# A hybrid HGRN2 and pooling trunk: the channel mixing of the last pooled group behind the first two column tiles of g, its gate in the larger pool of tiles

## The chip, the core and the metric

The kernel runs on one core of a Trainium2 chip. The metric is the device time of one execution in microseconds (us); lower is better. The engines are TensorE (PE, with its weight loads PEld), VectorE (DVE), ScalarE (ACT), GpSimd (POOL) and SyncE (SP), which issues most of the loads.

## What is computed

The reference is one layer of a trunk with two token mixers on the same normalised input, 512 tokens by 2048 channels. Cut to what matters here:

```python
proj = h @ w_in[l]
q_a, f_a, v_a, z_a, v_b, z_b, g_a, g_b = jnp.split(proj, IN_SPLITS, axis=-1)
o_a = hgrn2_mixer(q_a, f_a, v_a, lb_all[l])
y_a = rms(o_a) * hgrn_norm[l] * jax.nn.silu(z_a)
y_b = pool_mixer(v_b, pool_w[l], pool_scale[l]) * jax.nn.silu(z_b)
merged = jax.nn.sigmoid(g_a) * (y_a @ w_proj_a[l]) + jax.nn.sigmoid(g_b) * (y_b @ w_proj_b[l])
x = x + gate * rmsnorm(merged @ w_out[l], norm_post[l])

# pool_mixer, group g of four, 256 channels each, window w in (2, 4, 8, 16)
pooled_g = trailing_mean(v_b[:, g], w) - v_b[:, g]
mixed_g = pooled_g @ pool_w[g]          # the channel mixing, 256 x 256
```

`hgrn2_mixer` is a gated linear recurrence over 8 heads of 128, worked in chunks of 64 tokens.

## The kernel before

Tiles hold 128 channels by 512 tokens. Products are in float32 precision by three matmuls: each factor is split into a rounded part `hi` and the rest `lo`, and `mm3` (L198) adds hi x hi, hi x lo and lo x hi. A piece of weights comes through `w_piece` (L181): a load on SyncE into a ring of four raw tiles, a cast to `hi` on ScalarE (L187), a subtraction to `lo` on VectorE or GpSimd in turn (L188), each into rings of four. `in2` (L347) makes two column tiles of the input projection from four pieces, `name_0`, `_4`, `_8` and `_12`, of 24 matmuls each: eight for each column tile's four rows of h, in threes.

TensorE runs its matmuls in the order in which the program writes them (L97 to 104). The other engines' rows are put in order by the scheduler when the program is built, by priority and by what each row waits for; on the chip each engine then follows its own fixed order. Two pools of tiles matter: `t_w` (10 tiles, tag "w", short-lived) and `t_s` (32 tiles, tag "s").

After the first half of the projection the eight heads of the recurrence, `hgrn(h)` (L387), run as generators in the gaps: `mm3` calls `tick`, and after D0 to D6 = 21, 11, 13, 10, 6, 5 and 6 calls the next step of the head in turn writes its few matmuls between those of the projection. The steps named here are, in this order: `po` (the pairs), `lv_2`, `lv_8` and `lv_32` (scores within blocks of 8, 32 and 64 tokens), `far`, `state`, `o`, and `ms` (the mean square). Before each, ScalarE takes exponentials (`E`, `qs`, `R`, `A`) and VectorE subtracts before and multiplies after them; `Y` and `X` are `R` and `A` times the small tile `G`, and `far` reads them. In `E_8`, `qs_8_0` and so on the number is the block size; with two numbers ahead (`E_5_8`) the first is the head.

In between come the four pooled groups (L849 to 853): `vb` of group gi by `in2`, the pooling sums in `pool_tile` (L590, to `pl_hi` and `pl_lo`), `zb` by `in2`, then `pool_group` (L609): the weights `pw`, for both halves m a silu of `zb` (`szb`, L614), six matmuls (`mix`, L618), the product `yb` (L620) and its store to DRAM by GpSimd (L621). Hgrn heads 3, 4 and 5 run beside groups 1, 2 and 3. Right behind group 3 begins g, `in2("g0_0")` (L879), then `za` (L874), whose silus gate the heads, and the rest of g, with a sigmoid on each tile (L894). Silu, exp, sigmoid, square root and logarithm are kept in different tables on ScalarE; where the table has to change, an ACT_TABLE_LOAD stands ahead of the activation.

Of the kernel before, what the change touches and what calls it, by code (L numbers as in the profile page):

```python
# [12 lines left out]
AF = mybir.ActivationFunctionType  # L13
# [21 lines left out]
def trunk(ctx, tc, x, c, w_ada, b_ada, norm_pre, norm_post, w_in, lower_bounds, hgrn_norm,  # L35
          pool_w, pool_scale, w_proj_a, w_proj_b, w_out, out):
    nc = tc.nc
# [15 lines left out]
    def t_s(name, dt=F32):  # L53
        return act.tile([P, S], dt, tag="s", bufs=32, name=name)

    def t_w(name, n=S, dt=F32):
        return act.tile([P, 544], dt, tag="w", bufs=10, name=name)[:, :n]

    def t_ps(name):
        return ps.tile([P, S], F32, tag="ps", name=name)  # L60
# [4 lines left out]
    def t_pg(name):  # L65
        return pg.tile([P, S], F32, tag="pg", name=name)
# [4 lines left out]
    def paced(hi):  # L71

        if wsum_steps:
            dst, src, kw = wsum_steps.pop(0)
            with tc.issue_after(last_pool[0]):
                t = ins_of(nc.gpsimd.tensor_copy(token, hi[:, 0, 0:1].bitcast(F32)))  # L76
            with tc.issue_after(t):
                last_pool[0] = ins_of(nc.gpsimd.dma_start(dst, src, max_dma_last_dim=1024, **kw))  # L78

    def load(dst, src):  # L80

        if last_load[0] is None:
            d = nc.sync.dma_start(dst, src)
        else:
            with tc.issue_after(last_load[0]):
                d = nc.sync.dma_start(dst, src)
        last_load[0] = ins_of(d)
# [4 lines left out]
    def ins_of(d):  # L92
        return getattr(d, "ins", d)
# [38 lines left out]
    def finish_heads(n):  # L132
        while steps and len(heads_done) < n:
            tick(1)
# [46 lines left out]
    def w_piece(name, src, k0, nk, c0, n, eng=None):  # L181

        raw = ring.tile([P, nk, n], F32, tag="raw", bufs=4, name=f"{name}_raw")
        load(raw, src[k0 * P:(k0 + nk) * P, c0:c0 + n].rearrange("(k p) n -> p k n", p=P))
        hi = ring.tile([P, nk, n], F32R, tag="whi", bufs=4, name=f"{name}_hi")
        lo = ring.tile([P, nk, n], F32R, tag="wlo", bufs=4, name=f"{name}_lo")
        last_w[0] = ins_of(nc.scalar.copy(hi, raw))  # L187
        (eng or (nc.gpsimd if steps and next(turn) else nc.vector)).tensor_sub(lo, raw, hi.bitcast(F32))  # L188
        paced(hi)
        return hi, lo  # L190
# [7 lines left out]
    def mm3(o, wh, wl, xh, xl, first, last):  # L198
        matmul(o, wh, xh, first, False)
        matmul(o, wh, xl, False, False)  # L200
        matmul(o, wl, xh, False, last)
        if in_order[0]:
            tick()
# [139 lines left out]
    def proj2(name, src, nk, c0, xh, xl, outs):  # L343
        for k0 in range(0, nk, 4):
            cols(f"{name}_{k0}", src, k0, 4, c0, xh, xl, outs, 0, nk - 1)

    def in2(name, c0):  # L347
        outs = [t_ps(f"{name}_ps0"), t_ps(f"{name}_ps1")]
        proj2(name, w_in, KT, c0, hh, hl, outs)
        return outs  # L350
# [227 lines left out]
    def gate_a(h, p):  # L578
        sz = t_w(f"sza_{h}")
        nc.scalar.activation(sz, p, AF.Silu)  # L580
        sz_a[h] = sz

    def finish_a(h):
        y = o_sb[h]
        nc.vector.scalar_tensor_tensor(y, y, vec[:, R_HN + h:R_HN + h + 1], sz_a[h], op0=ALU.mult, op1=ALU.mult)
        last_pool[0] = ins_of(nc.gpsimd.dma_start(y_dram[0][h], y))
# [3 lines left out]
    def pool_tile(i, p):  # L590

        w = WINDOWS[i // 2]
        v = t_w(f"vb_{i}", 528)
        nc.vector.memset(v[:, 0:16], 0.0)
        nc.scalar.copy(v[:, 16:528], p)
        cur, n, lo = v, 1, 0
        while n < w:
            nxt = t_w(f"vb_{i}_{n}", 528)
            lo += n
            nc.vector.tensor_add(nxt[:, lo:528], cur[:, lo:528], cur[:, lo - n:528 - n])  # L600
            cur, n = nxt, 2 * n
        if w > 1:
            nc.vector.scalar_tensor_tensor(cur[:, 16:16 + w - 1], cur[:, 16:16 + w - 1], float(w),
                                           inv_pos[:, 0:w - 1], op0=ALU.mult, op1=ALU.mult)
        pl = t_w(f"pl_{i}")
        nc.vector.scalar_tensor_tensor(pl, cur[:, 16:528], 1.0 / w, v[:, 16:528], op0=ALU.mult, op1=ALU.subtract)
        pooled[i] = split(f"pl_{i}", pl, t_s)

    def pool_group(gi, zp):  # L609
        hi, lo = w_piece(f"pw_{gi}", pool_w[gi], 0, 2, 0, 256)  # L610
        for m in range(2):
            i = 2 * gi + m
            sz = t_w(f"szb_{i}")
            nc.scalar.activation(sz, zp[m], AF.Silu)  # L614
            mx = t_pg(f"mix_{i}")
            for k in range(2):
                ph, pl = pooled[2 * gi + k]
                mm3(mx, hi[:, k, m * P:(m + 1) * P], lo[:, k, m * P:(m + 1) * P], ph, pl, k == 0, k == 1)  # L618
            y = t_w(f"yb_{i}")
            nc.vector.scalar_tensor_tensor(y, mx, vec[:, R_PS + i:R_PS + i + 1], sz, op0=ALU.mult, op1=ALU.mult)  # L620
            nc.gpsimd.dma_start(y_dram[1][i], y)  # L621
# [3 lines left out]
    def gate_rows(j, k):  # L625

        if k == 0:
            gate[j] = t_w(f"gate_{j}")
        t = t_w(f"gw_{j}_{k}")
        load(t, w_ada[k * P:(k + 1) * P, 2 * D + j * S:2 * D + (j + 1) * S])  # L630
        if k == 0:
            nc.vector.tensor_scalar(gate[j], t, c_act[:, 0:1], None, op0=ALU.mult)
        else:
            nc.vector.scalar_tensor_tensor(gate[j], t, c_act[:, k:k + 1], gate[j], op0=ALU.mult, op1=ALU.add)  # L634

    def gate_finish(j):

        acc = gate[j]
        br = t_w(f"bg_{j}")
        load(br[0:1, :], b_ada[:, 2 * D + j * S:2 * D + (j + 1) * S])  # L640
        nc.vector.tensor_add(acc[0:1, :], acc[0:1, :], br[0:1, :])
        np_b = t_w(f"npost_{j}")
        load(np_b, norm_post[:, j * S:(j + 1) * S].to_broadcast([P, S]))
        gp = t_pg(f"gate_ps_{j}")
        hi, lo = split(f"gate_{j}", acc, lambda name, dt: t_w(name, S, dt))
        matmul(gp, ones_v, hi, True, False)
        matmul(gp, ones_v, lo, False, True)
        nc.vector.scalar_tensor_tensor(acc, gp, float(P), np_b, op0=ALU.mult, op1=ALU.mult)
# [195 lines left out]
    for h in (4, 6):  # L844
        o2 = in2(f"q{h}", OFF_Q + h * P)
# [3 lines left out]
    for gi in range(4):  # L849
        o2 = in2(f"vb{gi}", OFF_VB + gi * 256)  # L850
        pool_tile(2 * gi, o2[0]); pool_tile(2 * gi + 1, o2[1])
        o2 = in2(f"zb{gi}", OFF_ZB + gi * 256)
        pool_group(gi, o2)


    HK = D // 2
# [13 lines left out]
    for b, off in ((0, OFF_GA), (1, OFF_GB)):  # L870
        for m in range(0, KT, 2):
            if (b, m) == (0, ZA_AT):
                for h in range(0, NH, 2):
                    o2 = in2(f"za{h}", OFF_ZA + h * P)  # L874
                    gate_a(h, o2[0]); gate_a(h + 1, o2[1])
                    if h < 6:
                        finish_heads(h + 2)
                        finish_a(h); finish_a(h + 1)
            o2 = in2(f"g{b}_{m}", off + m * P)  # L879
            if (b, m) == (0, ZA_AT + 2):  # L880
                finish_heads(NH)
                finish_a(6); finish_a(7)

            first = ZA_AT // 2 + 2
            step = b * KT // 2 + m // 2 - first
            for i in range(max(0, step * GATE_PER), min(4 * KT, (step + 1) * GATE_PER)):
                gate_rows(i // KT, i % KT)
                if i % KT == KT - 1:
                    gate_finish(i // KT)
            if (b, m) == (0, ZA_AT + 2):  # L890
                wsum_steps += wsum_later
            for r in range(2):
                sig[b][m + r] = t_s(f"sig{b}_{m + r}")
                nc.scalar.activation(sig[b][m + r], o2[r], AF.Sigmoid)  # L894
# [220 lines left out]
```

## Time and profile before

| | |
|---|---|
| time, median of 3 runs | 1358.65 us (1358.01 to 1361.25) |
| profiled execution, own time | 1361.33 us |
| its span in the trace | 1359.4 us |
| TensorE busy | 1317.6 us (97%) |
| VectorE busy | 812.0 us (60%) |
| ScalarE busy | 558.9 us (41%) |
| GpSimd busy | 343.6 us (25%) |
| mean granted clock of TensorE | 0.992 |

The trace holds one execution. Its times count from the start of the span; the 1.9 us between the span and the execution's own time lie around it. A row of a timeline gives the start, the duration, the engine and line, the operation, what it writes and reads, how many alike it holds, and in brackets the idle time ahead of it with what ended it. Matmuls overlap: one of 512 columns is shown as 0.39 us long while the next begins 0.23 us after it. The granted clock is TensorE's, as a share of 2.4 GHz; 0.50 is its lower level of 1.2 GHz.

### The profile page before, as it was taken

What the parts mean: (1) busy time and instruction counts of PE and PEld (TensorE: products, weight loads), DVE (VectorE), ACT (ScalarE), POOL (GpSimd) and SP (SyncE); (2) the same over time, 40 slices, a digit from 0 to 9 for tenths busy, and PEclk for the clock granted to TensorE, in tenths of its full rate; (3) what the DMA queues carried; (4) which work ended last, traced back from release to release, by engine and by line L of the source; (5) the groups of instructions that cost most, each with busy time, mean ns of one, the idle gap of its engine ahead of it and who ended that gap; (6) DMA issues with size and microseconds to landing.
All of it is one profiled execution on the core that took longest, in us unless ns stands there. A gap on an engine that the chain in (4) does not pass through costs nothing.

```text
span 1359.4 us, 16610 instructions
## 1 busy us (share of the span) xinstructions
PE 1317.6 (97%) x6031; PEld 1087.5 (80%) x6031; DVE 812.0 (60%) x1336; ACT 558.9 (41%) x787; POOL 343.6 (25%) x381
## 2 busy tenths in 40 slices
PE   4999999999999999999999999999999999999995
PEld 2777788888888888788888888888888888888884
DVE  4679654347669696786843443444245545596757
ACT  5634453353545645465642222122242222265552
POOL 2545511222322332222302323232454100000020
PEclk9989999999999999999999999999999999999998
DMA  9979733322132323323238899998899633356683
GB/s 311 357 237 357 256 95 105 87 70 92 54 118 62 117 75 104 109 66 124 95 105 266 253 270 260 250 261 289 244 236 221 156 95 93 97 182 188 198 313 137
DMA packets 182266, 238.13 MB, mean 175 GB/s; under 512 B 9548, under 2 KB 137636, under 8 KB 182184
## 3 DMA queue, kind: packets, MB, share of 16 engines
q1 hardware_dynamic: 155528, 188.78, 43.6%
q0 software_dynamic: 25344, 46.14, 14.7%
q10 hardware_dynamic: 1312, 2.14, 0.4%
q8 instruction: 47, 0.77, 0.2%
q14 instruction: 35, 0.29, 0.1%
HBM read 228.64 MB, written 41.94 MB: 199 GB/s over the span
## 4 chain that ended last, share of the span: by engine, by line
PE 85%; DVE 3%; ACT 0%; issue 0%; POOL 0%; DVEq 0%; ACTq 0%
PE g_ps L101 26%; PE out L101 10%; PE vb_ps L101 6%; PE za_ps L101 6%; PE v_ps L101 6%; PE pb L101 6%; PE pa L101 6%; PE zb_ps L101 5%; PE q_ps L101 3%; PE g L101 3%; PE lv L101 2%; PE o L101 1%; PE mix L101 1%; DVE og L1040 1%; DVE vb L600 1%; PE po L101 0%
## 5 line engine op out<-in xcount | busy, mean ns | idle before, releaser
L101 PE MATMUL g_ps<-h_hi,g_hi 128*128 128x512 f32 x512 | 200.3, 391 | 0.0
L101 PE MATMUL g_ps<-h_hi,g_lo 128*128 128x512 f32 x512 | 199.6, 390 | 0.0
L101 PE MATMUL g_ps<-h_lo,g_hi 128*128 128x512 f32 x512 | 199.5, 390 | 0.0
L187 ACT CAST g_hi<-g_raw 128x1024 fp32r<-128x1024 f32 x64 | 67.1, 1050 | 177.5 <-PE g_ps L101 115.4
L101 PEld LDWEIGHTS g_ps<-h_hi,g_lo 128*128 128x128 f32 x512 | 96.1, 188 | 20.1
L101 PEld LDWEIGHTS g_ps<-h_hi,g_hi 128*128 128x128 f32 x512 | 96.2, 188 | 19.9
L101 PEld LDWEIGHTS g_ps<-h_lo,g_hi 128*128 128x128 f32 x512 | 96.2, 188 | 19.8
L188 DVE TENSOR_TENSOR g_lo<-g_raw,g_hi 128x1024 fp32r<-128x1024 f32 x61 | 74.0, 1220 | 59.5 <-ACT g_hi L187 59.5
L634 DVE SCALAR_TENSOR_TENSOR gate<-gw,c_act,gate 128x512 f32<-128x512 f32 x60 | 45.0, 751 | 95.8 <-DMA gw<-in_w_ada_dram 94.9
L188 DVE TENSOR_TENSOR wo_lo<-wo_raw,wo_hi 128x1024 fp32r<-128x1024 f32 x56 | 68.4, 1225 | 40.4 <-ACT wo_hi L187 40.3
L187 ACT CAST wo_hi<-wo_raw 128x1024 fp32r<-128x1024 f32 x56 | 59.0, 1053 | 61.0 <-PE out L101 48.2
L76 POOL COPY token<-g_hi 128x1 f32<-128x1 f32 x52 | 36.8, 709 | 183.6 <-ACT g_hi L187 183.5
L115 DVE SCALAR_TENSOR_TENSOR ada_acc<-ada,c_act,ada_acc 128x512 f32<-128x512 f32 x104 | 73.2, 753 | 8.1 <-DMA ada<-in_w_ada_dram 7.1
L1049 POOL DMA_DIRECT2D xr<-in_x_dram x16 | 8.7, 546 | 242.4 <-PE out L101 242.4
L78 POOL DMA_DIRECT2D wsum<-in_w_out_dram x48 | 52.9, 1105 | 4.4 <-issue 4.3
L101 PE MATMUL out<-wo_lo,op_hi 128*128 128x512 f32 x128 | 50.6, 395 | 3.4 <-DVE wo_lo L188 3.4
L101 PE MATMUL vb_ps<-h_hi,vb_hi 128*128 128x512 f32 x128 | 51.5, 402 | 0.0
L101 PE MATMUL za_ps<-h_hi,za_hi 128*128 128x512 f32 x128 | 51.1, 400 | 0.0
L101 PE MATMUL zb_ps<-h_hi,zb_hi 128*128 128x512 f32 x128 | 51.0, 398 | 0.0
L101 PE MATMUL out<-wo_hi,op_hi 128*128 128x512 f32 x128 | 50.6, 395 | 0.0
L101 PE MATMUL v_ps<-v_hi,h_hi 128*128 128x512 f32 x128 | 50.5, 395 | 0.0
L101 PE MATMUL out<-wo_hi,op_lo 128*128 128x512 f32 x128 | 50.5, 394 | 0.0
(346 smaller groups left out, 3389.3 us busy)
## 6 DMA issues: line engine op xcount, KB each, us to landing
ada<-in_w_ada_dram SPq DMA_DIRECT2D x128, 256.0 KB, 6.6
g_raw<-in_w_in_dram SPq DMA_DIRECT2D x64, 512.0 KB, 4.9
wsum<-in_w_out_dram POOLq DMA_DIRECT2D x48, 512.0 KB, 7.7
gw<-in_w_ada_dram SPq DMA_DIRECT2D x64, 256.0 KB, 8.6
wo_raw<-wsum SPq DMA_DIRECT2D x32, 512.0 KB, 4.2
wo_raw<-in_w_out_dram SPq DMA_DIRECT2D x24, 512.0 KB, 4.2
v_raw<-in_w_in_dram SPq DMA_DIRECT2D x16, 512.0 KB, 3.6
vb_raw<-in_w_in_dram SPq DMA_DIRECT2D x16, 512.0 KB, 3.6
```

The lines of the kernel that those rows point to most:

```text
L76: t = ins_of(nc.gpsimd.tensor_copy(token, hi[:, 0, 0:1].bitcast(F32)))
L78: last_pool[0] = ins_of(nc.gpsimd.dma_start(dst, src, max_dma_last_dim=1024, **kw))
L101: d = nc.tensor.matmul(o, lhsT, rhs, start=start, stop=stop, skip_group_check=onto)
L115: d = f(*args, **kw)
L187: last_w[0] = ins_of(nc.scalar.copy(hi, raw))
L188: (eng or (nc.gpsimd if steps and next(turn) else nc.vector)).tensor_sub(lo, raw, hi.bitcast(F32))
L600: nc.vector.tensor_add(nxt[:, lo:528], cur[:, lo:528], cur[:, lo - n:528 - n])
L634: nc.vector.scalar_tensor_tensor(gate[j], t, c_act[:, k:k + 1], gate[j], op0=ALU.mult, op1=ALU.add)
L1040: nc.vector.scalar_tensor_tensor(og[t][j], og[t][j], ro, xr[t][j], op0=ALU.mult, op1=ALU.add)
L1049: nc.gpsimd.dma_start(xr[t][j], x[t * P:(t + 1) * P, j * S:(j + 1) * S])
```

## The change

`pool_group` becomes a generator. Both silus are issued first, into tiles of the pool "s" where they were in "w", and a pause follows; the mixing, the products and the stores come behind the pause. For groups 0 to 2 it is resumed at once, so that their matmuls stay where they were. For group 3 it is resumed behind the first `in2` of g, ahead of `ms` of hgrn 5. The weights `pw_3` keep one place in the rings of four until then.

```diff
--- before.py
+++ after.py
@@ -608,10 +608,12 @@
 
     def pool_group(gi, zp):
         hi, lo = w_piece(f"pw_{gi}", pool_w[gi], 0, 2, 0, 256)
+        szs = [t_s(f"szb_{2 * gi + m}") for m in range(2)]
         for m in range(2):
-            i = 2 * gi + m
-            sz = t_w(f"szb_{i}")
-            nc.scalar.activation(sz, zp[m], AF.Silu)
+            nc.scalar.activation(szs[m], zp[m], AF.Silu)
+        yield
+        for m in range(2):
+            i, sz = 2 * gi + m, szs[m]
             mx = t_pg(f"mix_{i}")
             for k in range(2):
                 ph, pl = pooled[2 * gi + k]
@@ -850,7 +852,10 @@
         o2 = in2(f"vb{gi}", OFF_VB + gi * 256)
         pool_tile(2 * gi, o2[0]); pool_tile(2 * gi + 1, o2[1])
         o2 = in2(f"zb{gi}", OFF_ZB + gi * 256)
-        pool_group(gi, o2)
+        mix = pool_group(gi, o2)
+        next(mix)
+        if gi < 3:
+            next(mix, None)
 
 
     HK = D // 2
@@ -877,6 +882,8 @@
                         finish_heads(h + 2)
                         finish_a(h); finish_a(h + 1)
             o2 = in2(f"g{b}_{m}", off + m * P)
+
+            next(mix, None)
             if (b, m) == (0, ZA_AT + 2):
                 finish_heads(NH)
                 finish_a(6); finish_a(7)
```

The number of operations stays the same, but for eight more ACT_TABLE_LOADs on ScalarE: two in group 2, three in group 3, one behind it at the sigmoids of hgrn 6, and two at the first gates of `za`. The other engines' rows stay as many. In hgrn 3 `vb2_0_lo` moves on VectorE from ahead of `Y` to behind `X`. The loads on SyncE keep their order.

ScalarE, beside group 3 (hgrn 5), before: `g0_0_8_hi` is the cast of the third piece of the first two tiles of g, `szb` the silus, `za0` the first gate tiles.

```order
L194 CAST pl_7_hi_4538<-pl_7_4536 128x512
L428 ACTIVATE E_5_8_4619<-E_5_8_4619 128x512
L440 ACTIVATE qs_5_8_0_4623<-qs_5_8_0_4623 128x384
L440 ACTIVATE qs_5_8_1_4631<-qs_5_8_1_4631 128x384
L187 CAST g0_0_8_hi_4867<-g0_0_8_raw_4865 128x1024
L187 CAST g0_0_12_hi_4902<-g0_0_12_raw_4900 128x1024
L481 ACTIVATE E_5_32_4690<-E_5_32_4690 128x512
L489 ACTIVATE R_5_4696<-R_5_4696 128x512
L504 ACTIVATE A_5_4710<-sg_5_4449 128x512
L614 ACT_TABLE_LOAD
L614 ACTIVATE szb_6_4732<-zb3_ps0_4542 128x512
L614 ACTIVATE szb_7_4744<-zb3_ps1_4543 128x512
```

And now, from the same row on:

```order
L194 CAST pl_7_hi_4538<-pl_7_4536 128x512
L428 ACTIVATE E_5_8_4619<-E_5_8_4619 128x512
L613 ACT_TABLE_LOAD
L613 ACTIVATE szb_6_4732<-zb3_ps0_4542 128x512
L440 ACT_TABLE_LOAD
L440 ACTIVATE qs_5_8_0_4623<-qs_5_8_0_4623 128x384
L440 ACTIVATE qs_5_8_1_4631<-qs_5_8_1_4631 128x384
L481 ACTIVATE E_5_32_4690<-E_5_32_4690 128x512
L613 ACT_TABLE_LOAD
L613 ACTIVATE szb_7_4733<-zb3_ps1_4543 128x512
L489 ACT_TABLE_LOAD
L489 ACTIVATE R_5_4696<-R_5_4696 128x512
```

The two silus moved from behind `A` to ahead of `qs_8_0` and of `R`, each with a load ahead and one behind it; `A` and the casts of `g0_0_8` and `g0_0_12` follow these rows, where the casts stood ahead of `E_32`.

VectorE at the same place, before: `sd` is the tile of scores into which `lv` is copied under masks.

```order
L480 TENSOR_TENSOR E_5_32_4690<-sg_5_4449 128x256
L488 TENSOR_TENSOR R_5_4696<-sg_5_4449 128x512
L188 TENSOR_TENSOR g0_0_8_lo_4868<-g0_0_8_raw_4865,g0_0_8_hi_4867 128x1024
L482 TENSOR_TENSOR E_5_32_4690<-k_5_4451,E_5_32_4690 128x256
L483 TENSOR_TENSOR E_5_32_4690<-q_5_2305,E_5_32_4690 128x256
L505 TENSOR_TENSOR A_5_4710<-q_5_2305,A_5_4710 128x512
L506 TENSOR_TENSOR R_5_4696<-k_5_4451,R_5_4696 128x512
```

And now, the rows that end at the same subtraction:

```order
L455 COPY_PREDICATED sd_5_4470<-mask_8_1_125,lv_5_8_0_4785 128x8x16
L455 COPY_PREDICATED sd_5_4470<-mask_8_1_125,lv_5_8_1_4791 128x8x16
L455 COPY_PREDICATED sd_5_4470<-mask_8_2_129,lv_5_8_0_4785 128x8x8
L455 COPY_PREDICATED sd_5_4470<-mask_8_2_129,lv_5_8_1_4791 128x8x8
L511 TENSOR_TENSOR Y_5_4798<-R_5_4696,G_5_4699 128x256
L511 TENSOR_TENSOR Y_5_4798<-A_5_4710,G_5_4699 128x256
L511 TENSOR_TENSOR X_5_4797<-R_5_4696,G_5_4699 128x128
L511 TENSOR_TENSOR X_5_4797<-A_5_4710,G_5_4699 128x128
L511 TENSOR_TENSOR X_5_4797<-R_5_4696,G_5_4699 128x128
L511 TENSOR_TENSOR X_5_4797<-A_5_4710,G_5_4699 128x128
L188 TENSOR_TENSOR g0_0_8_lo_4829<-g0_0_8_raw_4826,g0_0_8_hi_4828 128x1024
L188 TENSOR_TENSOR za0_0_lo_5004<-za0_0_raw_5001,za0_0_hi_5003 128x1024
```

`g0_0_8_lo` moved from behind the difference for `R` to behind the copies of `lv_8`, `Y` and `X`; the products of `E_32`, `R` and `A` stand ahead of these rows.

ScalarE behind group 3, from the first sigmoid of g to the exponentials of hgrn 6 (`sg`, `k`, `l1`, `kp`), before:

```order
L395 ACTIVATE k_6_4952<-saved_B_2_486 128x512
L894 ACTIVATE sig0_1_4997<-g0_0_ps1_4765 128x512
L565 ACT_TABLE_LOAD
L565 ACTIVATE sq_5_4922<-ms_5_4946,eps_t_87 128x512
L403 ACT_TABLE_LOAD
L403 ACTIVATE l1_6_4957<-l1_6_4957 128x512
L404 ACTIVATE sg_6_4950<-sg_6_4950 128x512
L187 CAST za0_12_hi_5119<-za0_12_raw_5117 128x1024
L187 CAST za2_0_hi_5195<-za2_0_raw_5193 128x1024
L409 ACT_TABLE_LOAD
L409 ACTIVATE kp_6_4963<-l1_6_4957 128x256
L410 ACTIVATE kp_6_4963<-l1_6_4957 128x256
```

And now:

```order
L565 ACT_TABLE_LOAD
L565 ACTIVATE sq_5_4914<-ms_5_4943,eps_t_87 128x512
L393 ACT_TABLE_LOAD
L393 ACTIVATE sg_6_4947<-saved_B_2_486 128x512
L395 ACTIVATE k_6_4949<-saved_B_2_486 128x512
L187 CAST za0_12_hi_5119<-za0_12_raw_5117 128x1024
L187 CAST za2_0_hi_5195<-za2_0_raw_5193 128x1024
L403 ACT_TABLE_LOAD
L403 ACTIVATE l1_6_4954<-l1_6_4954 128x512
L404 ACTIVATE sg_6_4947<-sg_6_4947 128x512
L187 CAST za2_4_hi_5225<-za2_4_raw_5223 128x1024
L409 ACT_TABLE_LOAD
```

The sigmoids `sg` and `k` of hgrn 6, which stood ahead of `sig0_1` and the square root of `ms`, now stand behind the root with a load of their own, and `za2_4_hi` is ahead of `kp`; on GpSimd `za0_12_lo` and `za2_4_lo` moved up with their casts, and on VectorE the reciprocal of the root is ahead of the products of `sg` and `k`. On TensorE the twelve `mix` matmuls moved from ahead of `g0_0` to between its last piece and `ms`, and every hgrn step of head 5 comes as many matmuls later in `g0_0`.

## Rows read from the trace of the kernel before

**Rows 1.** The page, part 4: shares of the chain that ended last, by engine.
```profile
PE 85%; DVE 3%; ACT 0%; issue 0%; POOL 0%; DVEq 0%; ACTq 0%
```

**Rows 2.** Waits of TensorE, whole span: total us, times, longest us.
```profile
PE mix L101 <- ACT pl_hi L194: 1.6, 1, 1.6
...
PE mix L101 <- DVE pl_lo L195: 0.3, 1, 0.3
```

**Rows 3.** Timeline of TensorE, 551 to 561: start us, us, what, idle time before.
```profile
551.24 0.39 PE L101 MATMUL mix<-pl_hi,pw_hi 128*128 128x512 f32 x1
...
556.42 0.39 PE L101 MATMUL g_ps<-h_hi,g_hi 128*128 128x512 f32 x1
...
559.82 1.47 PE L101 MATMUL lv<-qs,E 128*128 128x192 f32 x8
...
560.99 0.53 PE L101 MATMUL g_ps<-h_hi,g_hi 128*128 128x512 f32 x1
```

**Rows 4.** Timeline of ScalarE, 553 to 565 (several alike in one row).
```profile
553.64 0.63 ACT L428 ACTIVATE E<-E 128x512 f32<-128x512 f32 x1
...
555.45 1.07 ACT L440 ACTIVATE qs<-qs 128x384 f32<-128x384 f32 x2 [1.18 <-DVE qs L438]
...
556.43 1.98 ACT L187 CAST g_hi<-g_raw 128x1024 fp32r<-128x1024 f32 x2
...
561.24 0.63 ACT L481 ACTIVATE E<-E 128x512 f32<-128x512 f32 x1 [2.83 <-DVE E L480]
...
563.02 1.28 ACT L614 ACT_TABLE_LOAD   x1
...
564.31 1.14 ACT L614 ACTIVATE szb<-zb_ps 128x512 f32<-128x512 f32 x2
```

**Rows 5.** Timeline of VectorE: rows that price an operation of an hgrn step.
```profile
505.10 1.29 DVE L455 COPY_PREDICATED sd<-mask,lv 128x192 f32<-128x192 int32 x6
...
507.52 0.41 DVE L511 TENSOR_TENSOR Y<-A,G 128x256 f32<-128x256 f32 x1
...
508.66 1.22 DVE L188 TENSOR_TENSOR vb_lo<-vb_raw,vb_hi 128x1024 fp32r<-128x1024 f32 x1
...
540.46 0.69 DVE L442 TENSOR_TENSOR qs<-q,qs 128x192 f32<-128x192 f32 x3
```

**Rows 6.** Timelines of GpSimd and VectorE where both work on two tiles.
```profile
443.42 3.35 POOL L188 TENSOR_TENSOR vb_lo<-vb_raw,vb_hi 128x1024 fp32r<-128x1024 f32 x1 [15.03 <-ACT vb_hi L187]
...
558.49 2.43 POOL L188 TENSOR_TENSOR g_lo<-g_raw,g_hi 128x1024 fp32r<-128x1024 f32 x1 [7.77 <-ACT g_hi L187]
...
558.73 2.48 DVE L480 TENSOR_TENSOR E<-sg 128x256 f32<-128x256 f32 x1
```

**Rows 7.** Timelines of VectorE and TensorE in groups 1 and 2.
```profile
443.27 1.22 DVE L188 TENSOR_TENSOR vb_lo<-vb_raw,vb_hi 128x1024 fp32r<-128x1024 f32 x1
...
446.36 0.39 PE L101 MATMUL vb_ps<-h_hi,vb_lo 128*128 128x512 f32 x1
...
509.24 0.71 PE L101 MATMUL far<-X 128*128 128x128 f32 x4
```

**Rows 8.** Timelines of TensorE and VectorE, from `ms` of hgrn 5 to `po` of hgrn 6.
```profile
583.80 0.40 PE L101 MATMUL ms<-sq_hi,ones_v 128*128 128x512 f32 x1
...
596.09 0.68 DVE L414 TENSOR_TENSOR kp<-k,kp 128x512 f32<-128x512 f32 x1
...
598.61 1.05 PE L101 MATMUL po<-qp,kp 128*128 128x128 f32 x8
```

**Rows 9.** A late wait of TensorE; stretches: us, busy us (instructions), granted clock, DMA share, GB/s.
```profile
1337.31 0.50 PE L101 MATMUL out<-wo_lo,op_hi 128*128 128x512 f32 x1 [3.38 <-DVE wo_lo L188]
...
71.00:79.00 8.00, 7.66 (x26) 0.57 1.08 360
...
552.00:556.00 4.00, 2.11 (x9) 1.00 0.39 124
...
1337.30:1341.52 4.22, 4.21 (x11) 0.60 0.00 0
```

## Prediction, written before the changed kernel was run

> **What bounds the kernel now.** I read the views in this order. The chain that ended last comes first: TensorE carries 85% of it [rows 1], so only what makes TensorE wait counts. Second are TensorE's waits: in the whole span two belong to the step that is moved, 1.6 us for `pl_hi` and 0.3 us for `pl_lo` [rows 2]. Third is TensorE's timeline at that place: the twelve `mix` matmuls fill 551.24 to 556.42, 5.18 us; at 0.2267 us a matmul (fifteen of `g` from 556.42 to 559.82) they need 2.72, so the stall costs 5.18 - 2.72 = 2.46 us from issue to issue [rows 3]. Last come ScalarE, VectorE and GpSimd beside it [rows 4 to 6], because the change also moves rows on these. The reader should see there that the weight splits (`hi` on ScalarE, `lo` on VectorE or GpSimd) and the hgrn steps share both engines in a fixed order, with little to spare.
>
> A measurement of this kernel can tell about 0.3%, 4.1 us, from no change. The best that the removed wait can give, 2.5 us, is less.
>
> **What is removed: -2.5 us.** With `mix` behind `g0_0` its operands are 20 us old when TensorE comes to them, so both waits go. The first two pieces of `g` are split as early as before, in the same places of each engine's order, so TensorE starts `g` at 551.24 with no new wait. The moved DMAs of `yb_6` and `yb_7` now stand on GpSimd behind `za0_4_lo` and behind the `G` copies; what they store is read only after all of `g`, so they cost nothing. The loads on SyncE keep their order; `g0_0` runs with three ring slots since `pw_3` keeps one, and SyncE's next raw slots come free with `lo` pieces that are needed earlier anyway: nothing.
>
> **What the silus in front add.** Silu needs another table than Exp. Before, both stood behind the step's exps and shared one load; now each stands between exps, with a load ahead and one behind. A load takes 1.28 us and the next activation starts 0.01 us after it (563.02 + 1.28, 564.31) [rows 4]. In group 3 there are four loads where there was one.
>
> *Term A, `lv_8` of hgrn 5.* TensorE comes to it after 27 matmuls: 551.24 + 27 x 0.2267 = 557.36. ScalarE: `E_8` ends at 554.27, load to 555.55, silu 0.57 (two take 1.14) to 556.1, load to 557.4, `qs_8_0` 0.53 to 558.0 [rows 4]; VectorE's three products 0.69 [rows 5], to 558.7, with hand-over 558.8. Stall 1.4 us (1.2 to 1.6). Before, `qs` began at 555.45.
>
> *Term B, `g0_0_8_lo`, the largest.* It moved on VectorE from ahead of the `E_32` products to behind everything of the step. TensorE is through `lv_8` (1.17 us) at 559.98, has 21 matmuls to the third piece (564.74), and needs this `lo` at the third of that piece's, 565.2 [rows 3]. ScalarE after `qs_8_1` (558.5): `E_32` to 559.0, load, silu, load to 562.2, `R` and `A` to 563.35, then casts of `g0_0_8` and `g0_0_12` to 564.3 and 565.25 [rows 4]. VectorE: two products to 564.15, six predicated copies 1.29 to 565.45, two `Y` and four `X` 1.47 (0.33 for the first `Y`, 1.14 from the second to the next row) to 566.9, `lo` 1.22 to 568.15 [rows 5]: stall 2.9 us. But GpSimd's `g0_0_12_lo` becomes ready at 565.25, just ahead of `Y`. Where GpSimd subtracts two tiles (2.43 us), a VectorE operation on two tiles stands still as long: 2.48 us for one of 256 columns, where another of that size takes 0.41 [rows 6, 5]. Then `Y` begins at 567.7, `lo` ends at 570.4: stall 5.2 us. I take 5.2, since in the trace the one that is ready first goes first; bounds 2.9 and 5.5.
>
> *Term C, group 1 (hgrn 3).* `vb2_0_lo` moved from before to behind `Y` and `X`. Before, it held off GpSimd's subtraction (ready at 443.42, 3.35 us long, 0.9 more than alone) [rows 6] and ended at 444.49; TensorE needs it at 446.36 [rows 7]. Now GpSimd gets in first, to 445.9 or so, then 1.47 and 1.22 follow: 448.3, a stall of 1.9. If VectorE's short rows keep ahead of GpSimd it is done by 446.1, with no stall. I take 1.8 (0 to 1.9).
>
> *Term D, group 2 (hgrn 4).* Two more loads delay the same products; `X` ended at 508.7 and `far` began at 509.24 [rows 5, 7], 0.5 us of room. I take 0.3 (0 to 0.4).
>
> *Term E, `po` of hgrn 6.* Before, `ms` was at 583.80, the last operand `kp` ended at 596.77 and `po` began at 598.61 [rows 8]: 1.84 us of room. Now the sigmoids of hgrn 6 stand behind the root of `ms` instead of ahead, which puts one more load (1.28), two activations (2 x 0.53) and the cast of `za2_4` (1.0, half of 1.98) into the chain from `ms` to `kp` [rows 4]: 3.3 - 1.8 = 1.5 us. GpSimd's `za0_12_lo` and `za2_4_lo` now fall beside the product with the root and beside the products of `qp`; each can hold VectorE 1.5 us longer, up to 4.5. I take one of the two: 3.0 (1.5 to 4.7).
>
> Sum of the stalls: 1.4 + 5.2 + 1.8 + 0.3 + 3.0 = 11.7 us.
>
> **Term F, the clock after a stall.** After TensorE stood 3.38 us at the end of the kernel, the granted clock was 0.60 over the next 4.22 us, most of it at the lower level of 1.2 GHz: 0.40 x 4.22 = 1.7 us lost. After its 1.6 us wait at `mix` the clock stayed 1.00 [rows 2, 9]. So B, certainly, and E, probably, cost 1.7 more each: 3.4 (0 to 6.8, by the row at 71 us, where 0.43 x 8 = 3.4 was lost after a lighter stretch) [rows 9].
>
> **Sum:** 11.7 + 3.4 - 2.5 = +12.6 us. The profiled execution took 1361.3, a span of 1359.4 and 1.9 around it; it would become 1373.9. It lies 2.7 above the median of 1358.65, and the stalls don't depend on that, so the forecast is 1358.65 + 12.6 = 1371.3 us.
>
> The Trainium skill ("ScalarE: Activation LUTs", section "What ACT_TABLE_LOAD costs") gives every switch of table 2.66 us: a load of 1283 ns and a drain of about 1380 ns. The trace has the load (1.28 us) but no drain: the row of the load at 563.02 names no idle time ahead of it, and silu follows within 0.01 [rows 4]. By the page A and B would grow by 1.38 for each of their four loads, 5.5 us, and the forecast would be about 1377.
>
> **The rivals.**
>
> 1. *The collisions on VectorE fall into gaps.* Then B is 2.9, C and D are 0, E is 1.5, A 1.2, and the clock drops once: 5.6 + 1.7 - 2.5 = +4.8, 1363.5 us. For it: the two engines are ready a few tenths apart, so a small shift lets VectorE's six short rows through first. Against it: at both places of [rows 6] one of the two is held up for most of the other's time.
> 2. *The stalls come, the clock stays.* 1371.3 - 3.4 = 1367.9. For it: the 1.6 us wait. Against it: the 3.38 us one.
> 3. *The loads are hidden (the other side).* ScalarE idles in this stretch, 2.83 us ahead of `E_32` alone [rows 4]. If the loads ran in such gaps, `R` and `A` would be ready by 560, `g0_0_8_lo` done before 565.2, and only the wait would go: 1358.65 - 2.5 = 1356.2 us, not to be told from no change. The point that decides is whether `g0_0_8_lo` ends before 565.2. Against it: a load stands in ScalarE's own queue, so the exps behind it wait, and the four loads on that path take 5.1 us, where there was none ahead of `R`; three of them would have to vanish.
> 4. *The drain of the page* is there when the table changes in both directions: 1377 us. The one row that can show it does not.
>
> **How the numbers follow.** Forecast 0.50; rival 1 0.18; rival 2 0.16; rival 3 0.11; rival 4 0.03; the remaining 0.02 for a gain elsewhere that I do not see. The range leaves out rival 3, rival 4 and the lower half of rival 1: from 1362 to 1376, the upper end being all terms at their upper bounds but the clock (1.6 + 5.5 + 1.9 + 0.4 + 4.7 + 3.4 - 2.5 = +15, 1373.7) and about 2 us for a longer clock drop. Slower by over 0.3% (above 1362.7): forecast, rivals 2 and 4, and two thirds of rival 1: 0.81. Within 0.3%: rival 3 and the rest of rival 1: 0.17. Faster: 0.02.
>
> **What would show it.** Right: no wait at `mix`; a wait of 1.4 us at `lv` for `qs` at about 557; one of 3 to 5 us at `g_ps` for `g_lo` at about 565, VectorE, with a long `Y` beside a GpSimd `g_lo`; one at `po` for `kp`; a granted clock under 1.00 just behind the long ones; eight more table loads. Wrong: if TensorE starts the third piece of `g0_0` on time, B and most of the sum fall; if `Y` takes 0.42 there, rival 1 holds.

## Result and profile after

The changed kernel takes 1373.55 us (median of 5, 1371.61 to 1375.33) beside 1360.91 for the kernel before on the same chip (median of 5, 1358.01 to 1361.87): a ratio of 1.0105, 95% interval 1.0093 to 1.0116, so slower by 1.1%: 12.6 us between the medians, 14.3 (12.7 to 15.8) by the ratio. The forecast was 1371.3 us, 1362 to 1376, with +12.6 us over the time before.

The profiled execution has a span of 1371.6 us, 12.2 more than that of before. Some of that is noise of the start: TensorE's waits for the first loads differ by about 1 us from run to run. Between the first matmul of `v_ps` and the first of `pa`, where no such wait lies, it went from 822.6 to 835.7 us: +13.1.

The page's part 4, shares of the chain that ended last, by engine:

```profile
PE 81%; DVE 5%; ACT 2%; issue 1%; POOL 0%; DVEq 0%; ACTq 0%
```

TensorE lost four points of the chain [rows 1], to VectorE and ScalarE. Its waits (total us, times, longest us):

```profile
PE g_ps L101 <- DVE g_lo L188: 4.5, 1, 4.5
PE po L101 <- DVE kp L414: 3.7, 1, 3.7
...
PE vb_ps L101 <- DVE vb_lo L188: 1.7, 1, 1.7
PE lv L101 <- DVE qs L442: 1.4, 1, 1.4
```

The two waits at `mix` [rows 2] are gone and four new ones have come; one of 3.4 us at `out`, left out here, was there before [rows 9]. TensorE's timeline at these places (start us, us, what, idle time before):

```profile
447.18 0.50 PE L101 MATMUL vb_ps<-h_hi,vb_lo 128*128 128x512 f32 x1 [1.69 <-DVE vb_lo L188]
...
551.94 0.39 PE L101 MATMUL zb_ps<-h_hi,zb_lo 128*128 128x512 f32 x1
552.17 0.39 PE L101 MATMUL g_ps<-h_hi,g_hi 128*128 128x512 f32 x1
...
559.82 1.54 PE L101 MATMUL lv<-qs,E 128*128 128x192 f32 x8 [1.37 <-DVE qs L442]
...
571.08 0.50 PE L101 MATMUL g_ps<-h_hi,g_lo 128*128 128x512 f32 x1 [4.46 <-DVE g_lo L188]
...
609.13 1.72 PE L101 MATMUL po<-qp,kp 128*128 128x128 f32 x8 [3.74 <-DVE kp L414]
```

g starts 0.23 us behind the last matmul of `zb`, without a pause, so the removed wait is fully gained. The idle time ahead of the four others is 1.69 + 1.37 + 4.46 + 3.74 = 11.26 us. Then the clock, as stretches from the end of each wait (us, busy us (instructions), granted clock, DMA share, GB/s):

```profile
447.00:452.00 5.00, 4.82 (x24) 1.00 0.86 285
...
559.80:564.80 5.00, 4.98 (x24) 1.00 0.00 0
...
571.08:576.08 5.00, 5.00 (x28) 0.66 0.83 256
...
609.13:614.13 5.00, 5.00 (x19) 0.66 0.21 71
```

Behind the two short waits the granted clock stayed 1.00; behind the two long ones it was 0.66 over five microseconds, part of them at 1.2 GHz: 0.34 x 5 = 1.7 us each. So 11.3 + 3.4 - 2.5 = 12.2 us; each wait costs some 0.15 us more from issue to issue (at `lv` the matmul ahead starts at 558.06, and 559.82 - 558.06 - 0.23 = 1.53 for 1.37 us of idle time), which makes 12.8, beside 13.1 in the stretch.

Where each wait comes from is seen on the other engines. ScalarE in group 3 (hgrn 5):

```profile
554.57 0.63 ACT L428 ACTIVATE E<-E 128x512 f32<-128x512 f32 x1
555.22 1.28 ACT L613 ACT_TABLE_LOAD   x1
556.52 0.60 ACT L613 ACTIVATE szb<-zb_ps 128x512 f32<-128x512 f32 x1
557.13 1.28 ACT L440 ACT_TABLE_LOAD   x1
558.43 0.94 ACT L440 ACTIVATE qs<-qs 128x384 f32<-128x384 f32 x2
```

The first silu stands between two exps and brings two loads; `qs`, which `lv` waits for, starts at 558.43 where it started at 555.45 [rows 4]. The second silu does the same ahead of `R` (loads at 559.90 and 561.81). In all the kernel has 59 loads, before 51. VectorE and GpSimd at the third piece of g:

```profile
566.18 0.42 DVE L511 TENSOR_TENSOR Y<-R,G 128x256 f32<-128x256 f32 x1
566.52 2.57 DVE L511 TENSOR_TENSOR Y<-A,G 128x256 f32<-128x256 f32 x1
...
569.82 1.21 DVE L188 TENSOR_TENSOR g_lo<-g_raw,g_hi 128x1024 fp32r<-128x1024 f32 x1
...
566.22 2.58 POOL L188 TENSOR_TENSOR g_lo<-g_raw,g_hi 128x1024 fp32r<-128x1024 f32 x1 [14.57 <-PE g_ps L101]
```

GpSimd's subtraction (the fourth piece, `g0_0_12`) began between the two `Y`: the first took 0.42, the second, of the same size, 2.57. Only then come `X` and the `lo` of the third piece, which ends at 571.03, and TensorE goes on at 571.08. The same in group 1, where `vb2_0_lo` now stands behind `Y`:

```profile
442.56 2.62 DVE L511 TENSOR_TENSOR Y<-R,G 128x256 f32<-128x256 f32 x1
...
442.36 2.54 POOL L188 TENSOR_TENSOR vb_lo<-vb_raw,vb_hi 128x1024 fp32r<-128x1024 f32 x1 [15.01 <-ACT vb_hi L187]
```

And ahead of `po` of hgrn 6, ScalarE, VectorE and GpSimd in turn:

```profile
593.21 1.28 ACT L393 ACT_TABLE_LOAD   x1
594.51 0.63 ACT L393 ACTIVATE sg<-saved_B 128x512 f32<-128x512 f32 x1
...
593.23 3.35 DVE L568 RECIPROCAL sq<-sq 128x512 f32<-128x512 f32 x1 [0.77 <-ACT sq L565]
...
596.80 2.62 DVE L397 TENSOR_SCALAR sg<-sg,oml,lb 128x512 f32<-128x512 f32 x1
599.35 0.68 DVE L569 TENSOR_TENSOR o<-o,sq 128x512 f32<-128x512 f32 x1
...
600.28 1.21 DVE L188 TENSOR_TENSOR za_lo<-za_raw,za_hi 128x1024 fp32r<-128x1024 f32 x1
...
605.74 1.70 DVE L413 TENSOR_TENSOR qp<-q,kp 128x256 f32<-128x256 f32 x1 [0.74 <-ACT kp L409]
...
596.74 2.40 POOL L188 TENSOR_TENSOR za_lo<-za_raw,za_hi 128x1024 fp32r<-128x1024 f32 x1 [4.72 <-ACT za_hi L187]
...
604.04 3.12 POOL L188 TENSOR_TENSOR za_lo<-za_raw,za_hi 128x1024 fp32r<-128x1024 f32 x1 [4.90 <-ACT za_hi L187]
```

The load and the sigmoids run beside the reciprocal of the root, which ends at 596.58. Behind it come the scalings of `sg` and `k` on VectorE (L397 among them), with a subtraction of `za` between. In the kernel before the sigmoids stood ahead of the root of `ms`, and the same L397 took a fifth of its time now. There it was the product with the root (L569) that stood still beside a subtraction on GpSimd:

```profile
584.07 0.55 DVE L397 TENSOR_SCALAR sg<-sg,oml,lb 128x512 f32<-128x512 f32 x1 [1.74 <-ACT sg L393]
...
590.89 2.89 DVE L569 TENSOR_TENSOR o<-o,sq 128x512 f32<-128x512 f32 x1
...
590.53 2.70 POOL L188 TENSOR_TENSOR za_lo<-za_raw,za_hi 128x1024 fp32r<-128x1024 f32 x1 [16.40 <-ACT za_hi L187]
```

From `ms` to the end of `kp` it took 12.97 us (583.80 to 596.77), now 18.79 (590.19 to 608.98).

### The profile page after: what moved, and what is told of

The parts are those of the page before. It is cut to its first block, busy times and chain, and to the rows that moved or that the text cites. A ratio compares the mean times of both kernels' runs of the same rounds, so it can differ in the third digit from the quotient of the medians.

```text
span 1371.6 us, 16609 instructions
## 1 busy us (share of the span) xinstructions
PE 1319.4 (96%) x6031; PEld 1088.2 (79%) x6031; DVE 810.5 (59%) x1336; ACT 569.9 (42%) x795; POOL 346.2 (25%) x381
## 4 chain that ended last, share of the span: by engine, by line
PE 81%; DVE 5%; ACT 2%; issue 1%; POOL 0%; DVEq 0%; ACTq 0%
PE g_ps L101 25%; PE out L101 10%; PE vb_ps L101 6%; PE v_ps L101 6%; PE pb L101 6%; PE pa L101 6%; PE za_ps L101 5%; PE zb_ps L101 4%; PE q_ps L101 3%; PE g L101 2%; PE lv L101 2%; PE o L101 1%; DVE vb L600 1%; DVE og L1047 1%; PE po L101 0%
## 5 line engine op out<-in xcount | busy, mean ns | idle before, releaser
L101 PE MATMUL vb_ps<-h_hi,vb_lo 128*128 128x512 f32 x128 | 50.3, 393 | 1.7 <-DVE vb_lo L188 1.7
```

What stands on the lines that cost most here:

```text
L101: d = nc.tensor.matmul(o, lhsT, rhs, start=start, stop=stop, skip_group_check=onto)
```

## Experiments

Each kernel is compared with the kernel before on the same chip. There are three questions: do the waits come from the larger pool, from the place of the mixing, or from both; are the causes named (table loads, the subtraction on GpSimd, the clock) the right ones; is the wait at `mix` to be had without them. Diffs are against the changed kernel.

**Silus first, mixing not moved (e1_silu_first).** All four groups resume at once.

```diff
-        if gi < 3:
-            next(mix, None)
+        next(mix, None)
```

> Both silus of a group first and in the larger pool, as in the change, but the mixing of group 3 stays ahead of g. Theory (the two parts cost together: early silus delay the exps, and the moved mixing brings TensorE to the hgrn steps 5 us sooner): the wait at mix stays 1.6 us, the one at vb_lo of group 1 is 1.7 us as in the change, none at lv_8, at the third piece of g or at po; 1 to 3 us slower than before. Rival (the early silus alone are the cost): waits at lv and at g_lo of 1 to 5 us, 8 us or more slower than before.

1362.71 us beside 1360.64, ratio 1.0018 [1.0004, 1.0032].

```profile
445.03 0.50 PE L101 MATMUL vb_ps<-h_hi,vb_lo 128*128 128x512 f32 x1 [1.69 <-DVE vb_lo L188]
```

The wait for `vb_lo` (term C) belongs to the pool: it is there with the mixing at its old place, and so is the wait at `mix` (1.57 us for `pl_hi`). A and B are not: TensorE comes to `lv` and to the third piece later by the twelve `mix` matmuls and the wait at them, and that is enough to cover the loads. One more wait of 0.44 us is at `far`. That the silus are issued first matters less than it looks: built with only the pool of `szb` exchanged, the kernel before gets the order of this run, row for row, on ScalarE, VectorE and GpSimd (it was not run).

**Mixing moved, silus as before (e2_move_only).** The silus go back behind the pause, into the small pool.

```diff
-        szs = [t_s(f"szb_{2 * gi + m}") for m in range(2)]
-        for m in range(2):
-            nc.scalar.activation(szs[m], zp[m], AF.Silu)
         yield
         for m in range(2):
-            i, sz = 2 * gi + m, szs[m]
+            i = 2 * gi + m
+            sz = t_w(f"szb_{i}")
+            nc.scalar.activation(sz, zp[m], AF.Silu)
```

> The mixing of group 3 moved as in the change, but each silu is issued with its own half of the mixing, in the small pool, as before. Theory: no wait at mix, none at vb_lo, lv_8 or the third piece of g; the silus now fall beside the square root of hgrn 5 with three loads more than before the change has there, so po of hgrn 6 waits some 5 to 7 us, and the clock drops behind it; 3 to 8 us slower than before. Rival (the move costs by itself, since pw_3 keeps a place in the rings): a wait of 3 to 5 us at g_lo of the third piece stays.

1364.31 us beside 1360.64, ratio 1.0033 [1.0019, 1.0047]: +4.5 us by the ratio. No wait at `mix`, `lv`, `g_ps` or `vb_ps`, but 3.79 us at `po` of hgrn 6 and 0.4 at `far`.

```profile
599.17 2.05 PE L101 MATMUL po<-qp,kp 128*128 128x128 f32 x8 [3.79 <-ACT E L428]
...
591.02 2.62 DVE L402 TENSOR_SCALAR sg<-sg 128x512 f32<-128x512 f32 x1
```

So term E comes with the new place of the mixing alone. The wait was smaller than expected. Three loads more than before stand between `ms` and `po`, but only the first is ahead of the root; the other two run beside the reciprocal. One collision came (L402, beside a subtraction of GpSimd), and by chance the sum is that of the changed kernel: 18.94 us from `ms` to `po` in both. The rival, that the place which `pw_3` keeps in the rings makes `g_lo` late, falls: there is no wait at `g_ps`.

**The larger pool for group 3 alone (e3_g3_alone).** Groups 0 to 2 keep their silus behind the pause, in the small pool.

```diff
-        szs = [t_s(f"szb_{2 * gi + m}") for m in range(2)]
-        for m in range(2):
-            nc.scalar.activation(szs[m], zp[m], AF.Silu)
+        szs = [None, None]
+        if gi == 3:
+            for m in range(2):
+                szs[m] = t_s(f"szb_{2 * gi + m}")
+                nc.scalar.activation(szs[m], zp[m], AF.Silu)
...
+            if sz is None:
+                sz = t_w(f"szb_{i}")
+                nc.scalar.activation(sz, zp[m], AF.Silu)
```

> The change for group 3 alone; groups 0 to 2 issue their silus as before. Theory: the waits at lv (1.4), g_lo (4.5) and po (3.7) as in the changed kernel, none at vb_lo (1.7 there); about 1.9 us faster than the changed kernel, 10 to 11 slower than before. Rival (the waits feed one another, so without the one at vb_lo the later ones grow): as slow as the changed kernel, 12 to 13 slower than before.

1370.26 us beside 1360.64, ratio 1.0077 [1.0055, 1.0099]. The wait for `vb_lo` is gone; those at `lv` (1.38 us), `g_ps` (4.48) and `po` (3.79) stay, with a clock of 0.66 and 0.68 behind the two long ones. So C is separate from the rest: the others don't change when it goes. Its price is the 1.69 us of the trace; the times (1.0105 against 1.0077 is 3.8 us, give or take 3) are too coarse to confirm it.

**The larger pool taken back, all else kept (e10_small_pool).**

```diff
-        szs = [t_s(f"szb_{2 * gi + m}") for m in range(2)]
+        szs = [t_w(f"szb_{2 * gi + m}") for m in range(2)]
```

> The change with one word undone: the silus first, the mixing of group 3 behind g0_0, but the gate in the small pool, as before. There a silu waits for one of ten buffers, and ScalarE's order has both behind R again. Theory (it is the larger pool that lets the silus in between the exps): no wait at vb_lo, lv or g_lo, at most 0.5 us at far; the wait at po (3.8) and the clock drop behind it (1.7) stay, since they come with the mixing's new place; 2 to 4.5 us slower than before. Rival (the pool doesn't matter, the silus are issued first in both): waits at lv and g_lo as in the changed kernel, 10 or more slower than before.

1362.79 us beside 1359.45, ratio 1.0027 [1.0015, 1.0040]. ScalarE in group 3:

```profile
556.33 0.63 ACT L489 ACTIVATE R<-R 128x512 f32<-128x512 f32 x1
556.98 1.28 ACT L613 ACT_TABLE_LOAD   x1
558.27 1.09 ACT L613 ACTIVATE szb<-zb_ps 128x512 f32<-128x512 f32 x2
```

Issued ahead of the pause as in the change, but in the pool of ten buffers, the silus stand behind `R` and share one load; the waits of A, B and C are gone, that of E (3.79 us at `po`) stays. It is the larger pool that lets the silus go early. Why is argued, not shown: in the small one a silu presumably has to wait until a buffer comes free, and by then the exps are through. With e2 this takes the change apart, by the ratios: the place alone +4.5 us (e2) or +3.7 (here), the larger pool alone +2.4 (e1), both together +14.3. They don't add up, because A and B need both: the early silus delay `lv` and the third piece, and the earlier g makes TensorE come to them before they are ready.

**No table to load (e4_no_tables).** A copy stands where the silu was, so the gate of the pooled branch is left out.

```diff
-            nc.scalar.activation(szs[m], zp[m], AF.Silu)
+            nc.scalar.activation(szs[m], zp[m], AF.Copy)
```

> The changed kernel with a copy of z_b where its silu was, in all four groups (the gate of branch B is left out), so that no table is loaded for it. Theory (the loads, and the places that the scheduler gives to the rows behind them, make the waits at lv and g_lo): both waits go, no load between E_8 and A; the wait at vb_lo of group 1 (1.7) and the one at po (3.7) stay with its clock drop; 3 to 6 us slower than before. Rival (the mixing's new place makes the waits, whatever ScalarE does): lv and g_lo wait as in the changed kernel.

1364.4 us beside 1359.28, ratio 1.0045 [1.0029, 1.0061].

```profile
551.09 0.58 ACT L613 ACTIVATE szb<-zb_ps 128x512 f32<-128x512 f32 x1
552.36 1.07 ACT L440 ACTIVATE qs<-qs 128x384 f32<-128x384 f32 x2 [0.69 <-DVE qs L438]
```

`szb` still stands early, between the exps, but without a load on either side, and the waits at `lv` and `g_ps` are gone: A and B need the loads. It doesn't split B further, since without loads the third piece's `lo` also stands earlier on VectorE again. C (1.70 us at `vb_ps`) and E (3.80 at `po`) stay: neither needs silu's table.

**The fourth piece's `lo` on VectorE (e5_g12_dve).** GpSimd has nothing to subtract beside `Y`.

```diff
-            cols(f"{name}_{k0}", src, k0, 4, c0, xh, xl, outs, 0, nk - 1)
+            cols(f"{name}_{k0}", src, k0, 4, c0, xh, xl, outs, 0, nk - 1, nc.vector if f"{name}_{k0}" == "g0_0_12" else None)
```

> The changed kernel, with the lo part of the fourth piece of g0_0 subtracted on VectorE (right behind that of the third) and not on GpSimd. Theory (GpSimd's subtraction held VectorE at Y for 2.1 us): Y takes 0.42 us, the wait at g_lo falls from 4.5 to 2.2 to 2.5 us, all else as in the changed kernel; 2 us faster than it if the clock still drops behind the wait, up to 3.7 if it does not. Rival (Y was late for another reason): the wait stays 4.5 us.

1371.04 us beside 1360.64, ratio 1.0084 [1.0063, 1.0104]. VectorE's second `Y`, TensorE at the third piece, and the clock behind it (lines of the helper moved by one):

```profile
567.77 0.42 DVE L512 TENSOR_TENSOR Y<-A,G 128x256 f32<-128x256 f32 x1
...
570.19 0.50 PE L101 MATMUL g_ps<-h_hi,g_lo 128*128 128x512 f32 x1 [2.31 <-DVE g_lo L189]
...
570.19:575.19 5.00, 5.00 (x28) 0.66 0.72 217
```

The second `Y` is back at 0.42 us and the wait shrinks by 4.46 - 2.31 = 2.15 us, all of what that `Y` had been held. So 2.15 us of B are the collision, and 2.31 the loads together with the later place of the third piece's `lo` (e4 removes both at once). The clock falls behind 2.31 us as it did behind 4.46. The two times are too near each other (1.0105 and 1.0084) to show 2 us by themselves; the trace shows them.

**TensorE kept busy through the two long waits (e6_busy).** Matmuls whose results nobody reads: 20 ahead of the matmul that waits for the third piece's `lo` (put in by the matmul helper, not shown), 16 ahead of `po` of hgrn 6.

```diff
+    def busy(n):
+        idle = t_pg("busy")
+        for i in range(n):
+            matmul(idle, hh[0][:, 0:P], hh[0], True, True)
...
+        if h == 6:
+            busy(16)
```

> The changed kernel, with 20 matmuls without use (512 columns, into a bank of their own) just ahead of the matmul that waits for g_lo, 4.5 us of work in a wait of 4.5, and 16 just ahead of po. Theory (each long wait costs about 1.6 us more through the clock): the waits shrink to a few tenths, the granted clock stays 1.00 behind both, and the kernel is 2 to 3.4 us faster than the changed one. Rival (the lower clock costs nothing, since what follows would wait anyway): the same time as the changed kernel.

1368.45 us beside 1359.28, ratio 1.0069 [1.0056, 1.0083].

```profile
563.95 4.69 PE L101 MATMUL busy<-h_hi 128*128 128x512 f32 x20
...
564.00:574.00 10.00, 10.00 (x58) 1.00 0.51 157
...
605.19:610.19 5.00, 5.00 (x26) 1.00 0.21 70
```

The stretch that TensorE can't use for the kernel's work stays, but the clock is 1.00 in it and behind it. The ratio falls from 1.0105 to 1.0069, some 4.9 us, give or take 2.4. The traces tell it more closely: from the matmul that waited for the third piece's `lo` to `ms` it is 17.56 us instead of 19.11, and from `po` of hgrn 6 to its `ms` 42.69 instead of 44.28, with no wait of TensorE inside either stretch. That is 1.55 + 1.59 = 3.1 us, where term F put 3.4: the price of the slower clock is real and apart from that of the wait.

**The gain without the price (f0_after_piece_0, f8_after_piece_2, f8w_small_pool).** Only group 3 is taken apart; its silus stand in the larger pool but are ordered behind `A`, the last exp of the step as the program writes it, and its mixing is resumed inside the first tiles of g: behind the first piece (f0) or behind the third (f8), so ahead of what belongs to `ms`.

```diff
+            if f"{name}_{k0}" == "g0_0_8":
+                next(mix_3[0], None)
...
-        nc.scalar.activation(A, L, AF.Exp)
+        last_A[0] = ins_of(nc.scalar.activation(A, L, AF.Exp))
...
+        if gi == 3:
+            for m in range(2):
+                szs[m] = t_s(f"szb_{2 * gi + m}")
+                with tc.issue_after(last_A[0]):
+                    nc.scalar.activation(szs[m], zp[m], AF.Silu)
```

In f0 the first line names `"g0_0_0"`.

> A version meant to beat both: the mixing of group 3 behind the first piece of g0_0 (24 matmuls) and not behind all four, so that every hgrn step keeps its place among the matmuls; the silus of group 3 forced behind the exp A of hgrn 5, in the larger pool; groups 0 to 2 as before. Theory: no wait at mix, as many table loads as before, and at most 0.8 us at far, since X ends at 566 to 567.5 and far comes at 566.8: 1.5 to 2.5 us faster than before. Rival (the hgrn chain sets the time of far, whatever is ahead of it): the 2.5 us come back as a wait at far or lv, the same time as before.

> The same with the mixing behind the third piece of g0_0. Theory: the same time as with the mixing behind the first, 1.5 to 2.5 us faster than before. Rival (the products yb on VectorE, which here stand behind the copies of lv_32, matter): up to 1.5 us between the two.

f0: 1357.6 us beside 1359.28, ratio 0.9986 [0.9977, 0.9994]. f8: 1356.55, ratio 0.9977 [0.9965, 0.9990]. Neither has a wait at `mix`, `lv`, `g_ps`, `far` or `po`, and both have 51 loads, as the kernel before. f8, TensorE and ScalarE:

```profile
538.39 1.06 PE L101 MATMUL po<-qp,kp 128*128 128x128 f32 x8
...
566.48 0.80 PE L101 MATMUL far<-X 128*128 128x128 f32 x4
...
559.42 0.63 ACT L492 ACTIVATE R<-R 128x512 f32<-128x512 f32 x1
560.07 1.28 ACT L619 ACT_TABLE_LOAD   x1
561.37 1.09 ACT L619 ACTIVATE szb<-zb_ps 128x512 f32<-128x512 f32 x2
```

On ScalarE `A` runs ahead of `E_32` and `R` in these builds, but the silus still come behind `R`, with one load for both. From `po` to `far` of hgrn 5 it takes 28.09 us, in the kernel before 30.40 (538.74 to 569.14): 2.3 us, the removed wait and nothing put in its place. By its ratio f8 is the fastest version of this study, 0.23% ahead of the kernel before (0.10 to 0.35%); from f0 its time is not told apart.

The last one tells whether f8 needs the larger pool and the forced order:

```diff
-                szs[m] = t_s(f"szb_{2 * gi + m}")
-                with tc.issue_after(last_A[0]):
-                    nc.scalar.activation(szs[m], zp[m], AF.Silu)
+                szs[m] = t_w(f"szb_{2 * gi + m}")
+                nc.scalar.activation(szs[m], zp[m], AF.Silu)
```

> The mixing of group 3 behind the third piece of g0_0, the silus of group 3 first and in the small pool, with no order forced on them; groups 0 to 2 as before. Theory (small pool and a place that leaves three pieces ahead and one behind are all that is needed): the same waits as the version with the forced order, none at mix, lv, g_lo, far or po, and 2 to 3 us faster than before. Rival (the forced order behind A was needed): waits at far or g_lo of 0.5 us or more, no gain.

1357.64 us beside 1359.45, ratio 0.9990 [0.9977, 1.0003]. TensorE's waits in its trace are those of f8, so the small pool does the ordering by itself; its time alone is not told apart from the kernel before, nor from f8.

## Why the prediction was right

The time lies in the range, and the mechanisms forecast are those that the traces show, but for the working of E. That the difference between the medians is 12.6 us, the forecast to the tenth, is luck: by the ratio it is 14.3, in the stretch of the trace 13.1, and B came 0.7 us smaller than put and E 0.7 larger.

- **The removed wait, -2.5:** as put. No wait at `mix`, g follows `zb` at once; f8 gains 2.3 us with no new wait in its place.
- **A, 1.4:** 1.37. The chain of a load, a silu and a second load ahead of `qs` was counted from rows, and e4 shows that without loads it is not there.
- **B, 5.2 (2.9 to 5.5):** 4.46. The collision came, but between the two `Y` and not ahead of both. The working let GpSimd be ready at 565.25 "just ahead of `Y`"; it was the other way round by 0.04 us for the first one (566.18 and 566.22), which so took its 0.42. Which of the two is held was a matter of hundredths of a microsecond. e5 splits B into 2.31 of loads and order, which the working put at 2.9, and 2.15 of collision, put at 2.3.
- **C, 1.8 (0 to 1.9):** 1.69, by the mechanism given, GpSimd first (442.36 against 442.56). The working's own sum is off: 445.9 + 1.47 + 1.22 is 448.6, a stall of 2.2 and not 1.9. e1 and e3 tie it to the pool alone.
- **D, 0.3 (0 to 0.4):** no wait at `far` of hgrn 4 in the changed kernel. In e10, where the rows around it stand otherwise, there are 0.19 us at this place.
- **E, 3.0 (1.5 to 4.7):** 3.74, in the range, but in part by other rows than the working names. This is the step that was mis-sized. The working added a load, two activations and a cast to the chain from `ms` to `kp`, 3.3 us, and one collision, 1.5, for which it had no row of that size. The load and the sigmoids cost nothing (593.21 to 595.66, beside the reciprocal). What grew the chain are the scalings of `sg` and `k`, the logarithms that need them and a subtraction of `za` on VectorE, all behind the reciprocal now, and a load for `kp` that has to wait for the cast of `za2_4`. Both collisions came, on L397 (2.62 instead of 0.55), a one-tile operation that the working had not considered, and on `qp` (1.70 instead of 0.42); but one had been there before, on the product with the root (2.89, now 0.68), which the working had not looked at. So of the 5.8 us by which the chain grew, collisions are 1.1 and the other rows 4.7; less the 1.84 of room it is 4.0, shown as 3.74 of idle time.
- **F, 1.7 behind each long wait:** 0.34 x 5 = 1.7 behind each, and e6 gives back 1.55 and 1.59. The bound "0 to 6.8" was too wide above: in these traces a drop cost 1.6 to 1.7 us behind waits of 2.31, 3.74, 3.79 (e2, e3) and 4.46 us, and 2.8 behind the 3.79 us of e10 (clock 0.50, 0.50 and 0.58 in the three stretches of 2 us behind `po`).

The rivals: 1 (collisions fall in gaps, 1363.5) falls by the long `Y`, and 3 (loads hidden, 1356.2) by the order of ScalarE: a silu that stands between exps makes the exps wait, and the point that decided is in TensorE's wait at `g_ps`, which wanted `g0_0_8_lo` at 566.62 (571.08 - 4.46) and got it at 571.03. 2 (the clock stays, 1367.9) falls by the two 0.66.

Rival 4, the drain, falls too. The exp at L428 begins at 554.57 and takes 0.63 us, so it ends at 555.20; the load starts at 555.22, ends at 556.50, and silu begins at 556.52. The Trainium skill ("ScalarE: Activation LUTs", section "What ACT_TABLE_LOAD costs") counts 2.66 us for every switch of table, about 1.38 of it a drain; in this trace a switch takes 1.30 us in one direction (555.22 to 556.52) and in the other (557.13 to 558.43), and the measurement decides.

## What to carry to other kernels

Before work is pulled forward on one engine, ask what its operations leave behind on the others: here a wait of 2.5 us was removed, and two silus, free to run early because their tiles came from a larger pool, switched the table of a ScalarE that was feeding TensorE with exps; and the new place of the mixing alone put rows of the next head behind a reciprocal (3.79 us at `po` in e2). A pool that is scarce can be what keeps an order; a larger one should come with that order written out (f8), or not at all (f8w). And a wait of TensorE is to be priced with the clock behind it: in these traces that was 1.6 to 2.8 us more behind the waits of 2.31 to 4.46 us, nothing behind those of 1.37 and 1.69.

## What the runs showed of the hardware

An operation of VectorE with one tile and per-partition scalars stood still beside a subtraction on GpSimd, just as those with two tiles did: L397 took 2.62 us instead of 0.55 beside GpSimd's 596.74 + 2.40, and in e2 L402, whose scalar is a constant, 2.62. The prediction had priced two-tile operations alone, though the kernel before shows one such row of one tile, in hgrn 2 (VectorE, then GpSimd):

```profile
353.44 2.97 DVE L402 TENSOR_SCALAR sg<-sg 128x512 f32<-128x512 f32 x1
...
353.11 2.56 POOL L188 TENSOR_TENSOR zb_lo<-zb_raw,zb_hi 128x1024 fp32r<-128x1024 f32 x1 [10.28 <-ACT zb_hi L187]
```

Its other instances there take 0.42 to 0.43. A group whose longest instance is seven times its median is worth a look before a collision is costed. The Trainium skill ("SBUF — State Buffer", section "Who interferes with whom") says that `tensor_scalar` can enter a mode that takes the ports shared with GpSimd, and that whoever issues first keeps them for the whole instruction; these rows agree, and so does the first `Y` at 566.18, which was issued 0.04 us ahead of GpSimd and was not held.
